# Gate projections with tokens on partitions, turned through DRAM; small transfers on GpSimd's queue; one square per tile

## The chip, the core and the metric

The kernel runs on one core of a Trainium2 chip, as one launch. The metric is device time in microseconds; the median of three runs before the change is 1785.23 us (1784.16 to 1788.43). The core has a matrix engine (PE, whose weight loads the profile lists as PEld), VectorE (DVE), ScalarE (ACT), GpSimd (POOL) and a sync engine (SP). DMAs are issued from the queues of SP, ACT and POOL. All engines run their own instruction streams in order and wait for each other through semaphores.

## The reference

Two layers over 256 latent tokens and 256 context tokens, all in float32 with 2048 channels. The first layer is the one that the change touches:

```
p  = h @ w_in                      # 256 x 14400: q, gate_a, z, k, v, x/B/C of the scan, dt
pc = hc @ w_in[:, COL_K:]
q, k = rms_norm over each head's 128 channels of p's q and k columns
ya = neighbourhood_attention(q, k, v, kc, vc, rpb) * silu(gate_a)      # 16 heads of 128
y_ssd = bidirectional_ssd(...)                                         # 8 groups of 4 heads of 64
yb = gated_group_rmsnorm(y_ssd + d * xs, z, g)      # y * silu(z), then a norm over each group's 256
x  = x + gate * (concat(ya, yb) @ w_out)
```

The second layer is a gated short convolution: `(silu(g) * bg * conv(cg * hv)) @ w_out`. The modulation rows (shift, scale, gate) of both layers come from a matrix-vector product with `ada_w`.

## The kernel before

**Precision.** Every large product is made from float32r halves: each operand is split into a high part (a cast) and a low part (what the cast lost), and three matmuls are summed, high by high, high by low and low by high. For a weight chunk of 128 x 1024 the cast `wH` is ACT's (line 427) and the subtraction `wL` is DVE's (line 434). Three chunks may be split ahead of use (`NW = 3`). `hH`, `hL` are the halves of the modulated input, `mix` those of the mixed heads before the output projection, `h` and `y` those of the second layer.

**Two layouts.** A projection is called with a kind. With `"act"`, `mm_act` puts tokens on partitions: an activation block of 128 x 128 is stationary, 512 weight columns move, and the result is a bank of 128 tokens x 512 channels for each 128 tokens. With a number, `mm_ws` puts channels on partitions: the weight block is stationary, and 256 or 512 tokens move. Q, K and V are projected with `"act"`; the scan's X and B with 512 moving tokens; C, the attention gate G and the scan's gate Z with 256 (only latent tokens have gates). The attention and the scan want gates with channels on partitions, in the tiles `gt` and `sz`, four blocks of 128 channels by 256 tokens. So Q and K have to be turned and G and Z need not.

**The turn through DRAM.** `kq_gen` squares Q or K on ACT head by head (four activations with an accumulated sum per tile), takes the power -1/2 on POOL, scales on DVE into `tmp` tiles with the 32-channel pieces shuffled (`mixed`, `plain`), and writes each tile to a DRAM scratch (`kqd`) by a DMA from POOL. `fetch` reads it back by four DMAs from POOL (line 214), each for 32 partitions, into the tile of tag `PT0`; `blocks` (line 219) finishes the turn with 32 x 32 block transposes on DVE. The same path turns the softmax's result (`ptd`, tile `D`) and, in the second layer, `trd` (tiles `Du`, `Dg`). All first-layer fetches share the one `PT0` buffer: `dfree` is true when it may be taken.

**Stages.** For a = 0 to 3 (four heads each) and s = 0 to 3 (two scan groups each), the first layer projects Q and K, then G and V, then C, X, Z of the scan; for a = 3 the scan comes between. Each projection's tail is a generator: `kq_gen`, `silu2_gen` (for G and Z: tanh on ACT, product on DVE, straight into `gt` or `sz`), `v_gen`, `head_gen` for one head, `make_x` and `group_gen` for the scan. A finished row block of `mix` whose place is still held by `hH` or `hL` is parked in DRAM (`put_mix`, `mixd`) and fetched later (`mix_gen`). `gemv_gen` makes the modulation rows on DVE (`acc`, line 826) in between and writes them to `mrow`. The parking, the modulation rows and the scan's decay rows (`csr`, `exr`) go by ACT's DMA queue (`DMA2`).

**What sets the order.** The program is written out while a planner (`Plan`) keeps a modelled clock for every engine. A generator yields what it needs next, `W_(engine, tiles)`, and `pump` emits the next step of the first generator in the queues `urgent`, `side`, `back` whose operands the model thinks ready in time. `cap` and `grow` change how many `tmp` and `half` tiles a generator may hold. The model decides only where an instruction stands in its engine's stream; on the chip semaphores decide when it runs.

Of the kernel before, what the change touches and what calls it, by code (L numbers as in the profile page):

```python
# [14 lines left out]
D = 2048  # L15
# [128 lines left out]
def kernel(ctx: ExitStack, tc, x, cx, ada_w, ada_b, w_in, w_out, sc_in, sc_out, rpb, small, const,  # L144
# [211 lines left out]
    def give(pool, *bs):  # L356
        pool.extend(bs)
# [451 lines left out]
    def gemv_gen():  # L809
        for n in range(16):  # L810
            lay = 0 if n < 4 else 1
            c0 = 4096 + n * 512 if n < 4 else (n - 4) * 512
            yield W_("SP")
            E(DMA.dma_start(adab[0:128:32, :], ada_b[lay, c0:c0 + 512].rearrange("(g c) -> g c", g=4)))
            for k in range(8):
                yield when(lambda: not (("gem", n, k) not in RAW))
                yield W_("DVE+", RAW["gem", n, k][1])
                raw, v = RAW.pop(("gem", n, k))
                ngem[0] -= 1
                for j in range(2):  # L820
                    if j:
                        yield W_("DVE", acc)
                    if not k + j:
                        E(V.tensor_scalar(out=acc, in0=v[:, j], scalar1=csil[:, 0:1], scalar2=None, op0=ALU.mult))
                        continue
                    E(V.scalar_tensor_tensor(out=acc, in0=v[:, j], scalar=csil[:, 2 * k + j:2 * k + j + 1], in1=acc,  # L826
                                             op0=ALU.mult, op1=ALU.add))
# [9 lines left out]
            yield W_("AQ", rowb)  # L837
            E(DMA2.dma_start(mrow[n // 4, (n % 4) * 512:(n % 4) * 512 + 512].rearrange("(g c) -> g c", g=4), rowb[0:128:32, :]))
            n_back[0] = n
            if n == 11:  # L840
                yield W_("AQ", mrow[2:3, 1024:])
                E(DMA2.dma_start(mrb[:32, :], mrow[1:3, :].rearrange("r (b c) -> (r b) c", c=128)))
# [132 lines left out]
    def kq_gen(key, a, ps, nt, stat, dst, banked):  # L975

        for t in range(nt):
            yield W_("ACT", ps[t])
            jk = tmp()
            for h in range(4):  # L980
                E(S.activation(jk[:, h * 128:h * 128 + 128], ps[t][:, h * 128:h * 128 + 128], AF.Square,
                               accum_out=stat[:, 4 * t + h:4 * t + h + 1]))
            give(free_t, jk)
        yield W_("DVE", stat)
        rstd(stat[:, :4 * nt], stat[:, :4 * nt], 128, EPS, 4 * nt)
        src = kqd[a, 512 * (key == "Q"):512 * (key == "Q") + 128 * nt]

        for t in range(nt):
            yield W_("DVE", stat)
            kn = tmp()  # L990
            E(V.tensor_tensor(out=mixed(kn), in0=plain(ps[t]),
                              in1=stat[:, 4 * t:4 * t + 4].unsqueeze(2).unsqueeze(3).to_broadcast([128, 4, 4, 32]), op=ALU.mult))
            if banked:
                give(free_b, ps[t])
            yield W_("POOL", kn)
            E(G.dma_start(src[t * 128:(t + 1) * 128], kn))
            give(free_t, kn)
# [12 lines left out]

    def v_gen(a, ps):
# [4 lines left out]
            give(free_b, ps[t])  # L1016
        got.add(("V", a))

    def silu2_gen(key, a, ps, dst, ok):
# [12 lines left out]
    b0 = rpbs[0, :, :]  # L1032
# [6 lines left out]
    def head_gen(a, h):  # L1039
# [32 lines left out]
        def scale_(qt):  # L1072
            yield W_("DVE", s4[:, 4 + qt:5 + qt])
            E(V.reciprocal(s4[:, 6 + qt:7 + qt], s4[:, 4 + qt:5 + qt]))
            yield W_("ACT", s4[:, 6 + qt:7 + qt])
            E(S.mul(sps[qt], sps[qt], s4[:, 6 + qt:7 + qt]))
            yield W_("POOL", sps[qt])
            E(G.dma_start(ptd[hd, qt * 128:(qt + 1) * 128], sps[qt]))
            give(free_t, sps[qt])
# [17 lines left out]
        yield from top(1, p1)  # L1097
        for qt in range(2):
            yield from scale_(qt)
        yield ("cap", 0, 0)  # L1100
# [43 lines left out]
    def dt_gen(ps):  # L1144
# [86 lines left out]
        yield W_("AQ", rw)  # L1231
        E(DMA2.dma_start(csr, rw[:64, 0:256]))
        E(DMA2.dma_start(exr, rw[:64, 256:512]))
        give(free_t, rw)
        got.add("dt")

# [251 lines left out]

    def do_g(a, nxt):
        psG = banks(2)  # L1490
        proj(512, 256, psG, nxt)
        spawn(urgent, silu2_gen("G", a, psG, gt, lambda: attn[0] >= 8 * a and (a or ("K", 0) in got)), 1)

    def do_ssd(s, nxt):
        if s:
            psB = banks(2)
            proj(256, 512, psB, 1)
            spawn(urgent, make_b(s, psB), 3)
        psC, = banks(1)
        proj(256, 256, [psC], 4)  # L1500
        spawn(urgent, make_c(s, psC), 0, 2)
        psX = banks(4)
        proj(512, 512, psX, 2)
        for gi in range(2):
# [3 lines left out]
        spawn(urgent, silu2_gen("Z", s, psZ, sz, lambda: ssd_done[0] >= 2 * s and ("K", 0) in got), 1)  # L1508
        for gi in range(2):
            spawn(side, group_gen(s, gi), 3, 4)  # L1510

# [39 lines left out]
    def mix_gen(ip):  # L1551
        two_ = (2 * ip, 2 * ip + 1)
        yield when(lambda: all(i in written or mH[i] is not None for i in two_) and free_rows[0] > (2 * ip + 1) % 16)
        mine = [i for i in two_ if mH[i] is None]
        if not mine:
            return
        yield ("grow", 1, 0)
        yield W_("AQ", *[mixd[i] for i in mine])
        mx = tmp()
        m3 = two(mx)  # L1560
        if len(mine) == 2:
            E(DMA2.dma_start(m3, mixd[2 * ip:2 * ip + 2].rearrange("b p c -> p b c")))
        else:
            E(DMA2.dma_start(m3[:, mine[0] % 2], mixd[mine[0]]))
# [221 lines left out]
    def row_gen(i, pC, pH):  # L1786
# [7 lines left out]
        for t in range(2):  # L1794
# [7 lines left out]
            give(free_t, ut)  # L1802
# [21 lines left out]
    def gate_gen(i, pB, pG):  # L1824
# [7 lines left out]
        for t in range(2):  # L1832
# [12 lines left out]
            give(free_t, o)  # L1845
# [114 lines left out]
```

## Time and profile before

| | |
|---|---|
| median of the runs | 1785.23 us |
| the profiled execution | 1781.03 us, span 1779.2 us |
| PE busy | 1736.7 us, 98% of the span |
| DVE, ACT, POOL busy | 1278.5, 799.0, 160.3 us (72%, 45%, 9%) |
| DMA | 412.51 MB, 232 GB/s over the span |
| chain that ended last | PE 71%, issue 10%, DMA 8%, DVE 7% |

"Busy" is the time in which at least one instruction of an engine ran. Consecutive matmuls overlap in the records, so the cost of a matmul in a stream is the distance between two starts, and not its own duration. The groups of instructions count by source line, operation and tile; most matmuls have line 200, since one helper records them all.

### The profile page before, as it was taken

How to read it: one execution, taken by the hardware profiler on the slowest of the kernel's cores; microseconds unless marked ns; L12 is line 12 of the kernel's file. 1: busy time of each engine (PE TensorE's matmuls, PEld its weight loads, DVE VectorE, ACT ScalarE, POOL GpSimd, SP SyncE). 2: the span in 40 equal slices, each digit the busy share in tenths (PEclk: the TensorE clock that was granted, in tenths of full speed). 3: DMA queues.
4: the chain of work that ended last, by engine and by line, in shares of the span. 5: the costliest groups of instructions: out<-in, count | busy, mean ns of one | idle time of the engine just before them, and what ended most of it. 6: DMA issues, size and time to landing. Idle time of an engine off the chain costs nothing.

```text
span 1779.2 us, 25400 instructions
## 1 busy us (share of the span) xinstructions
PE 1736.7 (98%) x9305; PEld 1445.1 (81%) x9305; DVE 1278.5 (72%) x2017; ACT 799.0 (45%) x1354; POOL 160.3 (9%) x245
## 2 busy tenths in 40 slices
PE   6999999999999999999999999999999999999998
PEld 4677988888788879788878898787878887878887
DVE  5566777878786876686887688776667776766555
ACT  5422444464344454343454445654435444444442
POOL 0000211012101012101012100010000000000000
PEclk9999999999999999999999999999999999999999
DMA  9987776677776678766578658777766887877775
GB/s 340 341 293 253 215 210 190 188 225 238 231 226 202 178 235 251 235 191 214 173 243 237 202 162 235 228 239 263 256 220 223 273 280 247 261 252 217 218 223 167
DMA packets 259742, 412.51 MB, mean 232 GB/s; under 512 B 35968, under 2 KB 105376, under 8 KB 259616
## 3 DMA queue, kind: packets, MB, share of 16 engines
q1 hardware_dynamic: 239888, 366.64, 66.5%
q0 software_dynamic: 12672, 37.76, 6.6%
q10 hardware_dynamic: 7056, 6.47, 1.1%
q8 instruction: 73, 1.20, 0.3%
q14 instruction: 53, 0.43, 0.1%
HBM read 386.53 MB, written 25.59 MB: 232 GB/s over the span
## 4 chain that ended last, share of the span: by engine, by line
PE 71%; issue 10%; DMA 8%; DVE 7%; POOL 2%; ACT 1%; SPq 1%; DVEq 0%; ACTq 0%; POOLq 0%
PE bank L200 70%; DMA raw<-in_ada_w 3%; DVE wL L434 2%; PE bank L204 1%; DMA raw<-in_w_in 1%; DMA dram_trd<-tmp 1%; DVE acc L826 1%; DMA bias<-dram_rpbs 1%; DMA kqD_K<-dram_kqd 1%; DMA D<-dram_ptd 1%; ACT wH L427 1%; DMA Du<-dram_trd 1%; POOL statk L576 0%; POOL kqD_K L214 0%; POOL Dg L214 0%
## 5 line engine op out<-in xcount | busy, mean ns | idle before, releaser
L427 ACT CAST wH<-raw 128x1024 fp32r<-128x1024 f32 (+1 forms) x440 | 459.4, 1045 | 650.9 <-PE bank L200 553.2
L434 DVE TENSOR_TENSOR wL<-raw,wH 128x1024 fp32r<-128x1024 f32 (+1 forms) x440 | 532.0, 1213 | 240.4 <-ACT wH L427 235.9
L200 PE MATMUL bank<-hH,wH 128*128 128x256 f32 (+1 forms) x1040 | 341.4, 328 | 0.9 <-ACT wH L427 0.9
L200 PE MATMUL bank<-hL,wH 128*128 128x256 f32 (+1 forms) x1040 | 337.2, 324 | 0.0
L200 PE MATMUL bank<-hH,wL 128*128 128x256 f32 (+1 forms) x1024 | 331.6, 324 | 0.6 <-DVE wL L434 0.6
L200 PE MATMUL bank<-wH,h 128*128 128x512 f32 x1024 | 318.4, 391 | 2.1 <-DVE h L1693 1.7
L200 PE MATMUL bank<-wH,hH 128*128 128x512 f32 x640 | 256.7, 402 | 4.8 <-ACT hH L767 2.6
L200 PE MATMUL bank<-wL,hH 128*128 128x512 f32 x640 | 250.5, 392 | 0.3 <-DVE wL L434 0.3
L200 PE MATMUL bank<-wH,hL 128*128 128x512 f32 x640 | 249.8, 391 | 0.1
L200 PEld LDWEIGHTS bank<-wH,h 128*128 128x128 f32 x1024 | 192.7, 188 | 44.3 <-DVE h L1693 3.0
L200 PEld LDWEIGHTS bank<-hH,wH 128*128 128x128 f32 x1040 | 198.1, 190 | 18.4 <-issue 2.0
L200 PEld LDWEIGHTS bank<-hL,wH 128*128 128x128 f32 x1040 | 198.2, 191 | 15.2
L826 DVE SCALAR_TENSOR_TENSOR acc<-raw,csil,acc 128x512 f32<-128x512 f32 x240 | 179.3, 747 | 41.1 <-DMA raw<-in_ada_w 37.3
L200 PEld LDWEIGHTS bank<-hH,wL 128*128 128x128 f32 x1024 | 194.9, 190 | 17.2 <-DVE wL L434 1.5
L200 PE MATMUL bank<-wL,h 128*128 128x512 f32 x512 | 200.4, 391 | 3.7 <-DVE wL L434 3.7
L200 PE MATMUL bank<-wH,mix 128*128 128x512 f32 x512 | 160.1, 390 | 0.0
L200 PEld LDWEIGHTS bank<-wH,hH 128*128 128x128 f32 x640 | 120.6, 188 | 36.5 <-issue 7.4
L200 PEld LDWEIGHTS bank<-wH,hL 128*128 128x128 f32 x640 | 120.5, 188 | 25.7 <-DVE hL L773 0.6
L200 PEld LDWEIGHTS bank<-wL,hH 128*128 128x128 f32 x640 | 120.6, 188 | 24.4 <-DVE wL L434 0.7
L200 PEld LDWEIGHTS bank<-wL,h 128*128 128x128 f32 x512 | 96.5, 188 | 25.3 <-DVE wL L434 5.3
L200 PEld LDWEIGHTS bank<-wH,mix 128*128 128x128 f32 x512 | 96.1, 188 | 20.2 <-issue 0.4
L200 PE MATMUL bank<-wL,mix 128*128 128x512 f32 x256 | 99.8, 390 | 0.0
(271 smaller groups left out, 1849.1 us busy)
## 6 DMA issues: line engine op xcount, KB each, us to landing
raw<-in_w_in SPq DMA_DIRECT2D x209, 512.0 KB
raw<-in_ada_w SPq DMA_DIRECT2D x163, 512.0 KB
raw<-in_sc_in SPq DMA_DIRECT2D x128, 512.0 KB
raw<-in_w_out SPq DMA_DIRECT2D x64, 512.0 KB
raw<-in_sc_out SPq DMA_DIRECT2D x32, 512.0 KB
dram_ptd<-tmp POOLq DMA_DIRECT2D x32, 256.0 KB, 4.1
D<-dram_ptd POOLq DMA_DIRECT2D x64, 128.0 KB, 4.9
tmp<-dram_csr SPq DMA_DIRECT2D x32, 256.0 KB
```

Of the source, the lines that this page charges most:

```text
L200: E(T.matmul(o, l, r, start=start, stop=stop, skip_group_check=True))
L204: E(T.transpose(o, i, ident if k == 128 else ident[:k, :k]))
L427: E(S.copy(H, v))
L434: E(V.tensor_tensor(out=Lo, in0=v, in1=H.bitcast(F32), op=ALU.subtract))
L826: E(V.scalar_tensor_tensor(out=acc, in0=v[:, j], scalar=csil[:, 2 * k + j:2 * k + j + 1], in1=acc, op0=ALU.mult, op1=ALU.add))
```

## The change

1. **G and Z are projected with `"act"`**, as Q and K are. `silu2_gen` makes the gate with tokens on partitions in `tmp` tiles, writes two tiles to a new DRAM scratch `gzd` from POOL, fetches them back into the `PT0` buffer by the four DMAs of `fetch`, and turns them by `blocks` on DVE into `gt` or `sz`. The columns of G and Z in `w_in` are permuted on the host so that the shuffle of 32-channel pieces is already made. `head_gen` takes `PT0` for its softmax only once its gate is there.
2. **ACT's DMA queue is no longer used**: the writes of `mrow`, its one read, the parked `mix` blocks and their reads, `csr` and `exr` are issued by POOL.
3. **One square per tile**: ACT squares a tile of 128 x 512 at once, DVE sums it per head.
4. **Tiles of a DMA are given back later**: a `tmp` or `half` tile that a POOL DMA reads counts as free only when the model has the DRAM tile written.

```
     def put_mix(i, o):
...
-        yield W_("AQ", o)
-        E(DMA2.dma_start(mixd[i], o))
+        yield W_("POOL", o)
+        E(G.dma_start(mixd[i], o))
+        yield W_("POOL", mixd[i])
         give(free_h, o)
...
     def kq_gen(key, a, ps, nt, stat, dst, banked):
...
-            for h in range(4):
-                E(S.activation(jk[:, h * 128:h * 128 + 128], ps[t][:, h * 128:h * 128 + 128], AF.Square,
-                               accum_out=stat[:, 4 * t + h:4 * t + h + 1]))
+            E(S.activation(jk, ps[t], AF.Square))
+            yield W_("DVE", jk)
+            E(V.tensor_reduce(out=stat[:, 4 * t:4 * t + 4], in_=four(jk), axis=AX.X, op=ALU.add))
...
     def silu2_gen(key, a, ps, dst, ok):
-        yield when(lambda: ok())
-        for b in range(2):
-            yield W_("ACT", ps[b])
+        ths = []
+        src = gzd[4 * (key == "Z") + a]
+        for t in range(2):
+            yield W_("ACT", ps[t])
             th = tmp()
-            E(S.activation(th, ps[b], AF.Tanh, scale=0.5))
+            E(S.activation(th, ps[t], AF.Tanh, scale=0.5))
             yield W_("DVE", th)
-            E(V.scalar_tensor_tensor(out=dst[:, 2 * b:2 * b + 2, :].rearrange("p b c -> p (b c)"), in0=th, scalar=1.0,
-                                     in1=ps[b], op0=ALU.add, op1=ALU.mult))
-            give(free_t, th)
-            give(free_b, ps[b])
+            E(V.scalar_tensor_tensor(out=th, in0=th, scalar=1.0, in1=ps[t], op0=ALU.add, op1=ALU.mult))
+            give(free_b, ps[t])
+            yield W_("POOL", th)
+            E(G.dma_start(src[t * 128:(t + 1) * 128], th))
+            ths.append(th)
+        yield W_("POOL", src)
+        give(free_t, *ths)
+        yield ("cap", 0, 0)
+        yield when(ok)
+        yield when(lambda: dfree[0])
+        Dt = d_take(f"D{key}{a}")
+        yield W_("POOL", src)
+        fetch(Dt, src)
+        for t in range(2):
+            yield W_("DVE+", Dt)
+            blocks(dst[:, :, t * 128:(t + 1) * 128], Dt[:, t])
+        dfree[0] = True
         got.add((key, a))
...
-        yield when(lambda: dfree[0] and (hd == 0 or ("d", hd - 1) in got))
+        yield when(lambda: dfree[0] and ("G", a) in got and (hd == 0 or ("d", hd - 1) in got))
...
-        proj(512, 256, psG, nxt)
+        proj(512, "act", psG, nxt)
...
-        proj(512, 256, psZ, nxt)
+        proj(512, "act", psZ, nxt)
...
     def mix_gen(ip):
...
-            E(DMA2.dma_start(m3, mixd[2 * ip:2 * ip + 2].rearrange("b p c -> p b c")))
+            E(G.dma_start(m3, mixd[2 * ip:2 * ip + 2].rearrange("b p c -> p b c")))
```

Three places show how the streams change. The first is PE at the border from the projection of K to that of G for a = 1. In the names `bank` is a PSUM bank, the operand after the arrow that comes first is the moving one, and the numbers are the tile's instance. Before:

```order
L200 MATMUL bank_123<-wH_138,hH_1437 128x512
L200 MATMUL bank_123<-wL_141,hH_1437 128x512
L200 MATMUL bank_123<-wH_138,hL_1442 128x512
L200 MATMUL bank_128<-hH_362,wH_136 128x256
L200 MATMUL bank_128<-hL_366,wH_136 128x256
L200 MATMUL bank_128<-hH_362,wL_139 128x256
```

After:

```order
L200 MATMUL bank_126<-wL_141,hH_1437 128x512
L200 MATMUL bank_126<-wH_138,hL_1442 128x512
L200 MATMUL bank_123<-wH_136,hH_362 128x512
L200 MATMUL bank_123<-wL_139,hH_362 128x512
L200 MATMUL bank_123<-wH_136,hL_366 128x512
```

For one block of 128 input channels, four times three matmuls of 256 columns became two times three of 512, with the operands' roles exchanged.

The second place is POOL's queue at the turn of Q and K for a = 1 (`kqD` are the fetches of Q and K, `D` those of a head, `DG` that of the gate, `ptd` and `gzd` writes of softmax tiles and gates, `r` and `statk` the powers -1/2). Before:

```order
L1467 TENSOR_TENSOR r_1_1706<-r_1_1706,const 128x2
L214 DMA kqD_Q_3809<-dram_kqd 32x8x128 x4
L214 DMA kqD_K_3867<-dram_kqd 32x8x128 x4
L214 DMA kqD_K_3922<-dram_kqd 32x8x128 x4
L1078 DMA dram_ptd<-tmp_113 128x512
L1078 DMA dram_ptd<-tmp_105 128x512
L214 DMA D_4055<-dram_ptd 32x8x128 x4
```

After:

```order
L1488 TENSOR_TENSOR r_0_1706<-r_0_1706,const 128x2
L959 DMA dram_mixd<-half_115 128x256
L214 DMA kqD_K_3497<-dram_kqd 32x8x128 x4
L959 DMA dram_mixd<-half_118 128x256
L214 DMA kqD_K_3587<-dram_kqd 32x8x128 x4
L1488 TENSOR_TENSOR r_1_1707<-r_1_1707,const 128x2
L838 DMA dram_mrow<-rowb 4x128
L959 DMA dram_mixd<-half_114 128x256
L214 DMA DG_3635<-dram_gzd 32x8x128 x4
```

A third fetch joins the two of K, parked blocks stand between them, and the power of a scan group now stands behind a fetch.

The third place is DVE at the same turn, where `KT` and `gt` are what the transposes fill, `acc` the modulation rows and `kL`, `qL` the first head's low parts. Before:

```order
L434 TENSOR_TENSOR wL_141<-raw_131,wH_138 128x1024
L219 STREAM_TRANSPOSE KT<-kqD_K_3867 128x4x4x32 x2
L826 SCALAR_TENSOR_TENSOR acc<-raw_132,csil,acc 128x512 x2
L826 SCALAR_TENSOR_TENSOR acc<-raw_134,csil,acc 128x512 x2
L434 TENSOR_TENSOR wL_139<-raw_133,wH_136 128x1024
L826 SCALAR_TENSOR_TENSOR acc<-raw_132,csil,acc 128x512 x2
L219 STREAM_TRANSPOSE KT<-kqD_K_3922 128x4x4x32 x2
```

After:

```order
L219 STREAM_TRANSPOSE KT<-kqD_K_3587 128x4x4x32 x2
L826 SCALAR_TENSOR_TENSOR acc<-raw_132,csil,acc 128x512
L434 TENSOR_TENSOR wL_139<-raw_131,wH_136 128x1024
L1106 TENSOR_TENSOR kL<-KT,kH 128x512
L1107 SCALAR_TENSOR_TENSOR qL<-QT,gqk,qH 128x256
L826 SCALAR_TENSOR_TENSOR acc<-raw_134,csil,acc 128x512 x2
L1083 ISA tmp_111,s_0_1694<-bank_123,bias_213 128x512
L1083 ISA s_0_1694 128x1
L1086 TENSOR_SCALAR s_0_1694<-s_0_1694 128x1
L826 SCALAR_TENSOR_TENSOR acc<-raw_132,csil,acc 128x512 x2
L219 STREAM_TRANSPOSE gt<-DG_3635 128x4x4x32 x2
L434 TENSOR_TENSOR wL_140<-raw_135,wH_137 128x1024
```

The gate's two transposes join the row of turns, directly ahead of a weight chunk's `wL`; between them and K's last pair stands one `wL` and the first head's work.

More of the change, by code (lines that the diff above doesn't have):

```diff
@@ L836, in gemv_gen @@
             give(free_b, ps)
-            yield W_("AQ", rowb)
-            E(DMA2.dma_start(mrow[n // 4, (n % 4) * 512:(n % 4) * 512 + 512].rearrange("(g c) -> g c", g=4), rowb[0:128:32, :]))
+            yield W_("POOL", rowb)
+            E(G.dma_start(mrow[n // 4, (n % 4) * 512:(n % 4) * 512 + 512].rearrange("(g c) -> g c", g=4), rowb[0:128:32, :]))
             n_back[0] = n
             if n == 11:
-                yield W_("AQ", mrow[2:3, 1024:])
-                E(DMA2.dma_start(mrb[:32, :], mrow[1:3, :].rearrange("r (b c) -> (r b) c", c=128)))
+                yield W_("POOL", mrow[2:3, 1024:])
+                E(G.dma_start(mrb[:32, :], mrow[1:3, :].rearrange("r (b c) -> (r b) c", c=128)))
                 yield W_("PE", mrb, nb=1)
@@ L996, in kq_gen @@
             E(G.dma_start(src[t * 128:(t + 1) * 128], kn))
-            give(free_t, kn)
+            kns.append(kn)
+        yield W_("POOL", src)
+        give(free_t, *kns)
         yield ("cap", 0, 0)
@@ L1099, in head_gen @@
             yield from scale_(qt)
+        yield W_("POOL", ptd[hd])
+        give(free_t, sps[0], sps[1])
         yield ("cap", 0, 0)
-        yield when(lambda: dfree[0] and (hd == 0 or ("d", hd - 1) in got))
+        yield when(lambda: dfree[0] and ("G", a) in got and (hd == 0 or ("d", hd - 1) in got))
         Dt = d_take(f"D{hd}")
@@ L1230, in dt_gen @@
         give(free_b, pr)
-        yield W_("AQ", rw)
-        E(DMA2.dma_start(csr, rw[:64, 0:256]))
-        E(DMA2.dma_start(exr, rw[:64, 256:512]))
+        yield W_("POOL", rw)
+        E(G.dma_start(csr, rw[:64, 0:256]))
+        E(G.dma_start(exr, rw[:64, 256:512]))
         give(free_t, rw)
@@ L1490, in do_g @@
         psG = banks(2)
-        proj(512, 256, psG, nxt)
-        spawn(urgent, silu2_gen("G", a, psG, gt, lambda: attn[0] >= 8 * a and (a or ("K", 0) in got)), 1)
+        proj(512, "act", psG, nxt)
+        spawn(urgent, silu2_gen("G", a, psG, gt, lambda: attn[0] >= 8 * a and (a or ("K", 0) in got)), 2)
     def do_ssd(s, nxt):
@@ L1506, in do_ssd @@
         psZ = banks(2)
-        proj(512, 256, psZ, nxt)
-        spawn(urgent, silu2_gen("Z", s, psZ, sz, lambda: ssd_done[0] >= 2 * s and ("K", 0) in got), 1)
+        proj(512, "act", psZ, nxt)
+        spawn(urgent, silu2_gen("Z", s, psZ, sz, lambda: ssd_done[0] >= 2 * s and ("K", 0) in got), 2)
         for gi in range(2):
@@ L1557, in mix_gen @@
         yield ("grow", 1, 0)
-        yield W_("AQ", *[mixd[i] for i in mine])
+        yield W_("POOL", *[mixd[i] for i in mine])
         mx = tmp()
@@ L1801, in row_gen @@
             E(G.dma_start(trd[2 * i, t * 128:(t + 1) * 128], ut))
-            give(free_t, ut)
+            cs[t] = ut
+        yield W_("POOL", trd[2 * i])
+        give(free_t, *cs)
         yield ("cap", 0, 0)
@@ L1844, in gate_gen @@
             E(G.dma_start(trd[2 * i + 1, t * 128:(t + 1) * 128], o))
-            give(free_t, o)
+            gs[t] = o
+        yield W_("POOL", trd[2 * i + 1])
+        give(free_t, *gs)
         yield ("cap", 0, 0)
@@ L1942 @@
     strict = np.stack([lt.T, lt], axis=1)
+    w_in = np.array(f('na_ssd_w_in')[0])
+    w_in[:, COL_G:COL_K] = w_in[:, COL_G:COL_K].reshape(D, 8, 4, 4, 32).transpose(0, 1, 3, 2, 4).reshape(D, 4096)
     arr = {
-        'x': f('x')[0], 'cx': f('ctx')[0], 'ada_w': f('ada_w'), 'ada_b': f('ada_b'), 'w_in': f('na_ssd_w_in')[0],
+        'x': f('x')[0], 'cx': f('ctx')[0], 'ada_w': f('ada_w'), 'ada_b': f('ada_b'), 'w_in': w_in,
         'w_out': f('na_ssd_w_out')[0], 'sc_in': f('sc_w_in')[0], 'sc_out': f('sc_w_out')[0], 'rpb': f('na_rpb')[0],
```

6 lines of the change are left out of this document (4 added, 2 removed).

## The prediction

> **What bounds the kernel now.** I read the page first, then PE's waits, then the distances of matmul starts in the timeline, then the queue that the change loads most, POOL.
>
> ```profile
> span 1779.2 us, 25400 instructions
> PE 1736.7 (98%) x9305; PEld 1445.1 (81%) x9305; DVE 1278.5 (72%) x2017; ACT 799.0 (45%) x1354; POOL 160.3 (9%) x245
> PEclk9999999999999999999999999999999999999999
> ...
> 175.00:1480.00 1305.00, 1292.41 (x6962) 1096.04 (x6961) 988.47 (x1580) 604.30 (x1081) 139.12 (x203) 1.00 0.73 223
> ```
>
> The last row is from the busy time by stretches: from 175 us, where the start-up ends, to 1480 us PE is busy for 1292.41 of 1305.00 us at the full granted clock (1.00). So PE bounds the kernel, only 12.6 us of that stretch are gaps, and time can be won in two ways: fewer or shorter matmuls, or those gaps. The waits of PE say what the gaps are:
>
> ```profile
> PE bank L200 <- DVE wL L434: 4.6, 7, 1.8
> PE bank L200 <- ACT qH L1085: 2.7, 2, 1.6
> PE bank L200 <- DVE tmp L1431: 2.3, 1, 2.3
> PE bank L200 <- DVE half L1454: 1.1, 1, 1.1
> PE bank L200 <- DVE PL L1115: 0.7, 2, 0.4
> ```
>
> They are few and short (total, times, longest): a late weight chunk here, a late first head there. DVE at 72% and ACT at 45% are not bounds, but PE depends on both in order.
>
> **The matmuls (the one term on the path).** How many there are of G's and Z's kind is in the groups by shape, and what one costs is the distance of starts:
>
> ```profile
> L200 PE MATMUL bank<-hH,wH 128*128 128x256 f32 x640 | 182.7, 286 | 0.0
> ...
> 299.83 0.28 PE L200 MATMUL bank<-hL,wH 128*128 128x256 f32 x1
> 302.95 0.28 PE L200 MATMUL bank<-hH,wH 128*128 128x256 f32 x1
> ...
> 389.65 0.39 PE L200 MATMUL bank<-wL,hH 128*128 128x512 f32 x1
> 398.72 0.39 PE L200 MATMUL bank<-wH,hL 128*128 128x512 f32 x1
> ```
>
> Between 299.83 and 302.95 us lie 26 distances in one unbroken stream of 256-column matmuls: 3.12/26 = 0.1200 us each. Between 389.65 and 398.72 us lie 40 distances of the "act" form with 512 columns: 9.07/40 = 0.2268 us each. Two of the short ones cost 0.2400, one long one 0.2268: 13.2 ns are saved per pair. The 640 matmuls of the row, times three halves, are 1920; C keeps 4 x 16 x 2 x 3 = 384 of them, so G and Z have 1536, which become 768 of 512 columns. 768 x 0.0132 = 10.2 us. Since PE is dense at both places, I count all of it as on the path.
>
> A rule of the Trainium skill speaks for less. Its page "TensorE: Matmul & The Clock Gate", section "Back-to-back issue gap", gives a warm matmul N/2.4 + 2.5 ns; by it 768 matmuls fewer would save only 768 x 2.5 ns = 1.9 us. The two rows differ by 106.8 ns for 256 columns, which agrees with the page's slope, but leave 13 ns, not 2.5, as the fixed part, so the measurement decides.
>
> **ACT.** The squares and the queue:
>
> ```profile
> L981 ACT ACTIVATE tmp<-bank 128x128 f32<-128x128 f32 x80 | 20.9, 308 | 0.0
> L981 ACT ACTIVATION_READ_ACCUMULATOR tmp<-bank 128x1 f32 x80 | 18.5, 240 | 0.0
> L605 ACT ACTIVATE tmp<-xs 128x512 f32<-128x512 f32 x8 | 5.0, 624 | 2.9 <-DMA xs<-in_x 2.7 <-DMA xs<-in_cx 0.2
> ACT wH L427 <- issue: 56.2, 25, 5.4
> ```
>
> The 80 squares and 80 reads of 20 tiles take 39.4 us, with the four tiles in `sz` and `gt` 47 us at the same price; 24 squares of 512 at 0.624 us take 15.0. ACT loses 32 us of work and 55 DMA issues. I cost it at nothing: ACT is idle over half of the time, and the cover stays. Whether the waits of the fourth row ("issue": ended by nothing that the profile shows, 25 times) were the queue's DMAs, and whether PE felt them, is open; PE's waits on ACT after the start-up are 2.7 (row of qH) and some below 1 us. Bounds 0 to -3 us; I take 0.
>
> **DVE.** It gets 16 block transposes and 24 sums of 128 x 512:
>
> ```profile
> L219 DVE STREAM_TRANSPOSE KT<-kqD_K 128x512 f32<-128x512 f32 x16 | 10.4, 689 | 10.5 <-DMA kqD_K<-dram_kqd 10.5
> L219 DVE STREAM_TRANSPOSE QT<-kqD_Q 128x512 f32<-128x512 f32 x8 | 5.2, 688 | 0.0
> L824 DVE TENSOR_SCALAR acc<-raw,csil 128x512 f32<-128x512 f32 x16 | 7.6, 475 | 3.8 <-DMA raw<-in_ada_w 3.8
> L826 DVE SCALAR_TENSOR_TENSOR acc<-raw,csil,acc 128x512 f32<-128x512 f32 x240 | 179.3, 747 | 41.1 <-DMA raw<-in_ada_w 37.3
> ```
>
> The transposes cost 16 x 0.689 = 11.0 us. No row shows a sum of 512; rows of that size lie between 475 and 747 ns, and I take the transpose's 0.689: 24 x 0.689 = 16.5 us. DVE comes to 1278.5 + 27.5 = 1306 us, 73%. The gate's own two operations stay as long as they were (the same 128 x 512). Cover: PE's work; if DVE were the bound of a stage, this would be the price, which is why the bounds are 0 and 27.5 us. Since PE's waits on `wL` add up to 4.6 us in seven times at 72% load, I take 0 for the work itself and put the waits into the next term.
>
> **POOL and the new turns.** POOL gets 16 writes and 32 fetch DMAs of gates, 24 parked blocks and 12 reads of them, 17 of the modulation rows and 2 of the decay rows: 103 DMAs.
>
> ```profile
> L214 POOL DMA_DIRECT2D D<-dram_ptd x64 | 37.7, 592 | 212.7 <-DVE PL L1115 102.5 <-DVE tmp L1372 58.5 <-issue 41.5
> L1078 POOL DMA_DIRECT2D dram_ptd<-tmp x32 | 17.9, 559 | 198.1 <-ACT tmp L1076 170.3 <-ACT tmp L1413 21.5 <-DMA raw<-in_w_in 4.0
> ```
>
> At 0.56 to 0.59 us each that is 60 us; POOL comes to 220 us, 12%. What counts is waiting in order, and the second layer shows it in one piece. POOL's rows, then DVE's, then PE's:
>
> ```profile
> 1473.03 1.77 POOL L214 DMA_DIRECT2D Du<-dram_trd  x3 [6.26 <-DMA dram_trd<-tmp]
> 1480.52 0.58 POOL L214 DMA_DIRECT2D Du<-dram_trd  x1 [5.72 <-issue]
> 1486.52 1.30 DVE L219 STREAM_TRANSPOSE u<-Du 128x512 f32<-128x512 f32 x2 [2.67 <-DMA Du<-dram_trd]
> 1493.17 2.35 DVE L434 TENSOR_TENSOR wL<-raw,wH 128x1024 fp32r<-128x1024 f32 x2
> 1494.45 0.50 PE L200 MATMUL bank<-wL,h 128*128 128x512 f32 x1 [1.79 <-DVE wL L434]
> ```
>
> Three DMAs of a fetch are issued at once, the fourth only 5.72 us later; the data land at 1486.4; DVE has stood for 2.67 us; the `wL` queued behind comes late, and PE stands for 1.79 us. Every new fetch can do this: behind the gate's transposes stand `wL` (the order's third place), on POOL the next head's fetch and a scan group's power. It need not:
>
> ```profile
> DVE KT L219 <- DMA kqD_K<-dram_kqd: 10.5, 4, 6.5
> DVE D L1109 <- DMA D<-dram_ptd: 7.4, 5, 2.7
> DVE u L219 <- DMA Du<-dram_trd: 5.2, 2, 2.7
> ```
>
> DVE waited at 4 of 8 fetches of K, 5 of 16 of a head, 2 of 4 of `u`, and at none of Q (0.0 in its row above). PE's waits that can come from a turn are `wL` 4.6, `qH` 2.7, `PL` 0.7, together 8.0 us, and there are 36 fetches: 0.22 us each. Bounds for one new fetch: 0 (as for Q) to 1.79 us (as above); for eight 0 to 14.3. I take 0.3 us each, a little over the mean, since G's and Z's fetches share one buffer and one queue with more DMAs than before: 2.4 us.
>
> The traffic, 8 x 1.05 MB written and read back in 412.5 MB, is 2% more at a DMA share of 0.73; SP's loads keep their order but for single places. I cost it at nothing: PE waited for a weight load from DRAM only in the start-up, which the change leaves as it was. Tiles held longer cost nothing by themselves either: they move where an instruction stands, and where one lacks, a side generator starts later behind PE's projections; without that cover it would show as a gap of the size of a landing, and such gaps are in the bounds above. The second layer's matmuls are untouched.
>
> **The sum.** 1781.0 (profiled execution) - 10.2 + 2.4 = 1773.2 us. The median of the runs is 4.2 us above the profiled execution, so in the runs 1785.2 - 7.8 = 1777.4, say 1777 us.
>
> **Rivals.**
>
> *More is won.* ACT's waits were the queue's and PE's small gaps go with them: besides the 10.2, `qH` 2.7 and `half`, `tmp` (1.1 and 2.3), none of it lost to new turns: 1785.2 - 10.2 - 6.1 = 1769 us. For it: 25 unexplained waits, on the engine that makes `wH`. Against: the gaps at these places name three engines.
>
> *The gain is eaten.* The new turns cost about 1 us each: 1785.2 - 10.2 + 8 = 1783 us, no change by the bound of 0.3% (5.4 us) that a measurement of this kernel can tell. For it: K, the fetch most like the new one (a buffer that is waited for, its transposes ahead of `wL`), had waits at half of its fetches.
>
> *Slower.* One mechanism: POOL's queue. The fourth DMA of a fetch waits until earlier ones are through, the writes now put ahead lengthen this, and everything on POOL behind it (a head's fetch, a group's power) comes late too. It decides if twelve fetches, the eight new ones and four old ones that now have a write directly ahead, cost the 1.79 us of the row: 21.5 us, so 1785.2 - 10.2 + 21.5 = 1796 us; slower by 0.3% from 15.6 us on. Against: POOL is at 12%, and a single write costs it 0.56 us. The Trainium skill speaks for it: "SBUF — State Buffer", section "SBUF: two separate sides", says that DMAs issued by GpSimd can starve for descriptors while DVE runs certain operations, and advises ACT's or SP's queue. The trace shows no slow issue, 592 ns on average beside a DVE at 72%; only the fourth waits.
>
> *The shapes cost alike.* If the 13 ns were not per matmul but of something that stays with G and Z (other operands, other neighbours), only the new turns would be left: 1785.2 + 2.4 = 1788 us. Against it stand 40 distances of the very form that is put in. The Trainium skill's formula above comes out near this case, with 1.9 us saved: 1786 us.
>
> **Chances and range.** My forecast, 1772 to 1780 us, 0.50; more is won 0.17; eaten 0.18; slower 0.11; the shapes cost alike 0.04. Faster by over 0.3% means below 1779.9: 0.48 of the first and all of the second, 0.65. Slower means above 1790.6: 0.11 and a hundredth of the others, 0.12. The rest, 0.23, is no change. The range leaves about 0.1 on each side: 1767, below the second case, to 1789, above "eaten" and "cost alike" and short of the slow one.
>
> **What would show it.** Right: 768 matmuls fewer, 512 columns at 0.227 us where 256 stood; PE's busy time from 175 to 1480 us down by some 10 us; POOL near 220 us; DVE near 1306, ACT near 767 us; waits of DVE on `DG` or `DZ` of a few us in all. Wrong: PE waits on `wL` or `qH` well over the 8 us above (the turns cost more), DVE's sums far over 0.75 us, gaps of PE behind POOL's powers, or a `kH,qH` product that stands earlier in PE's stream than its K can be there.

## The result and the profile after

The changed kernel takes 1797.27 us (median, 1790.3 to 1800.98) against 1784.7 us before: a ratio of 1.0068, 95% interval [1.0049, 1.0087]. It is slower by 12 us; forecast was 1777 us. The profiled execution took 1798.02 us, 17.0 us more than the one of before. From the page and from the busy time by stretches of after (columns: window, length, busy time of PE, PEld, DVE, ACT, POOL, granted clock, DMA share, GB/s):

```profile
span 1796.2 us, 23892 instructions
PE 1736.8 (97%) x8537; PEld 1411.1 (79%) x8537; DVE 1304.2 (73%) x2057; ACT 785.6 (44%) x1186; POOL 219.8 (12%) x348
...
175.00:1480.00 1305.00, 1273.74 (x6095) 1046.14 (x6094) 995.74 (x1597) 581.45 (x904) 193.88 (x298) 0.99 0.74 224
```

768 matmuls have gone, yet PE is busy as long as before, and the gaps from 175 to 1480 us have grown from 12.6 to 31.3 us. I split the distances of all matmul starts: if each is set to the median of its kind (tile names and shape), the sum falls from 1680 to 1670 us, by 10 us; what is over that by more than 0.25 us at a time, stalls, rises from 36.5 to 55.6; excesses of 0.03 to 0.25 us rise from 52.7 to 59.7. So the matmuls' gain is there, and 26 us were lost beside it. PE's waits of after (total, times, longest):

```profile
PE bank L200 <- DVE wL L434: 10.5, 14, 2.5
PE bank L200 <- ACT Vt L1019: 7.1, 1, 7.1
PE bank L200 <- DVE tmp L1452: 3.6, 5, 1.3
PE bank L200 <- ACT qH L1104: 3.5, 1, 3.5
PE bank L204 <- POOL r L1488: 3.1, 1, 3.1
```

`wL` has gone from 4.6 to 10.5, and three single stalls of 3 to 7 us are new. The longest shows how a stall comes about. POOL, then DVE, ACT and PE, in the timeline of after (start, duration, and in brackets the idle time before):

```profile
1128.25 0.76 POOL L1583 DMA_DIRECT2D tmp<-dram_mixd  x1
1135.87 0.72 POOL L1583 DMA_DIRECT2D tmp<-dram_mixd  x1 [6.87 <-issue]
1135.68 0.71 DVE L1130 STREAM_TRANSPOSE D<-D 128x512 f32<-128x512 f32 x1 [7.40 <-DMA D<-dram_ptd]
1137.69 1.06 ACT L1134 CAST PH<-D 128x1024 fp32r<-128x1024 f32 x1 [10.26 <-DVE D L1130]
1148.93 2.02 ACT L1019 COPY Vt<-bank 128x512 f32<-128x512 f32 x4
1149.56 1.19 PE L200 MATMUL bank<-tmp,xtm 128*64 128x128 f32 x8 [7.11 <-ACT Vt L1019]
```

DVE stood 7.4 us for a head's `D`, ACT stood 10.3 us for DVE, and the copies of `Vt` that free V's banks stood behind that in ACT's order; PE waited 7.1 us for them. POOL's wait of 6.87 us stands behind that `D` and not ahead of it: the fetch's fourth DMA was issued at 1126.25 us and landed 9.3 us later, while its other three had landed after 2.6 to 3.4 us. PE then ran at half clock:

```profile
1149.00:1150.00 1.00, 0.44 (x4) 0.44 (x6) 0.00 (x0) 1.00 (x4) 0.02 (x1) 0.50 0.89 211
1150.00:1152.00 2.00, 2.00 (x11) 1.48 (x8) 0.00 (x0) 1.58 (x3) 1.99 (x3) 0.50 0.72 231
```

The records of the granted clock show 0.5 for 3.4 or 6.8 us at a time, mostly at stalls of 1.8 us or more. Between 175 and 1700 us that is 7 us in all before and 27 us after. Half of the difference, 10 us, is the most that it can have cost by this estimate; of the small excesses, 2.9 us lie in such stretches before and 9.4 us after, which is most of the 7 us by which they rose. The Trainium skill, "TensorE: Matmul & The Clock Gate", section "What's actually happening", describes such a gate, with an activity window of about 3.4 us; the lengths of the stretches agree. It lets the clock fall after an idle window of that length, and here stalls of 1.8 us (before, at 1494 us) and 2.5 us (after, at 245 us) were enough.

### The profile page after: what moved, and what is told of

It reads as the page before. It is cut to its first block, busy times and chain, and to the rows that moved or that the text cites. A ratio compares the mean times of both kernels' runs of the same rounds, so it can differ in the third digit from the quotient of the medians.

```text
span 1796.2 us, 23892 instructions
## 1 busy us (share of the span) xinstructions
PE 1736.8 (97%) x8537; PEld 1411.1 (79%) x8537; DVE 1304.2 (73%) x2057; ACT 785.6 (44%) x1186; POOL 219.8 (12%) x348
## 5 line engine op out<-in xcount | busy, mean ns | idle before, releaser
L200 PE MATMUL bank<-wH,hH 128*128 128x512 f32 x896 | 360.3, 403 | 4.8 <-ACT hH L767 2.6
L200 PE MATMUL bank<-wL,hH 128*128 128x512 f32 x896 | 351.9, 393 | 0.8 <-DVE wL L434 0.8
L200 PE MATMUL bank<-wH,hL 128*128 128x512 f32 x896 | 351.3, 393 | 0.1
L200 PEld LDWEIGHTS bank<-wH,hH 128*128 128x128 f32 x896 | 169.8, 190 | 45.7 <-issue 6.6
L200 PE MATMUL bank<-hH,wH 128*128 128x512 f32 (+1 forms) x528 | 195.6, 370 | 0.9 <-ACT wH L427 0.9
L200 PE MATMUL bank<-hH,wL 128*128 128x512 f32 (+1 forms) x512 | 187.4, 366 | 5.9 <-DVE wL L434 5.9
L200 PE MATMUL bank<-hL,wH 128*128 128x512 f32 (+1 forms) x528 | 192.7, 365 | 0.0
L200 PEld LDWEIGHTS bank<-hH,wL 128*128 128x128 f32 x512 | 97.2, 190 | 23.3 <-DVE wL L434 7.8
L200 PEld LDWEIGHTS bank<-hH,wH 128*128 128x128 f32 x528 | 100.3, 190 | 18.0 <-issue 2.0
L200 PEld LDWEIGHTS bank<-hL,wH 128*128 128x128 f32 x528 | 100.4, 190 | 14.9
```

The costliest lines, as they stand in the source:

```text
L200: E(T.matmul(o, l, r, start=start, stop=stop, skip_group_check=True))
```

## Experiments

Ratios are to the kernel before, run beside each, so rows are compared by their ratios; the medians come from several chips. 0.1% is 1.8 us. All rows marked "2k" have the doubled DMA scratch of the first experiment. Seven kernels leave out the gates' turn or its DMAs, so that `gt` and `sz` hold no turned gate: `ring2k_noturn`, `noturn_traffic`, `order_alone` and the four whose names begin with `act_`.

| kernel | median us | ratio, 95% interval |
|---|---|---|
| after_ring2k (2k) | 1786.72 | 1.0018 [1.0006, 1.0030] |
| before_ring2k (2k) | 1785.16 | 1.0007 [0.9993, 1.0021] |
| no_queue | 1806.71 | 1.0128 [1.0110, 1.0147] |
| no_gates | 1780.97 | 0.9982 [0.9967, 0.9998] |
| gates_only | 1802.93 | 1.0127 [1.0098, 1.0155] |
| ring2k_traffic (2k) | 1802.74 | 1.0138 [1.0106, 1.0171] |
| ring2k_knows (2k) | 1784.56 | 1.0018 [1.0003, 1.0033] |
| ring2k_r260 (2k) | 1786.47 | 1.0033 [1.0013, 1.0053] |
| ring2k_noturn (2k) | 1789.07 | 1.0024 [1.0003, 1.0044] |
| noturn_traffic (2k) | 1789.06 | 1.0027 [1.0017, 1.0037] |
| no_gates_ring2k (2k) | 1777.47 | 0.9960 [0.9946, 0.9974] |
| no_gates_traffic (2k) | 1779.82 | 0.9985 [0.9970, 1.0000] |
| act_direct (2k) | 1769.95 | 0.9938 [0.9915, 0.9960] |
| act_transposes (2k) | 1788.09 | 1.0031 [1.0014, 1.0047] |
| order_alone (2k) | 1788.59 | 1.0040 [1.0020, 1.0061] |
| act_direct_unplanned (2k) | 1771.60 | 0.9941 [0.9924, 0.9959] |
| act_direct_r260 (2k) | 1775.73 | 0.9969 [0.9952, 0.9986] |
| ring2k_blind (2k) | 1792.65 | 1.0055 [1.0033, 1.0078] |

**1. The room for POOL's DMAs.** The order of every engine stays as it was.

```
-    sb.tile([128, 224], F32, tag="pad", name="pad", bufs=1)
+    sb.tile([128, 4], F32, tag="pad", name="pad", bufs=1)
-    nc = bacc.Bacc("TRN2", ..., dynamic_dma_scratch_size=1024)
+    nc = bacc.Bacc("TRN2", ..., dynamic_dma_scratch_size=2048)
```

> The changed kernel with POOL's DMA scratch doubled from 1024 to 2048 (an unused filler tile gives the room); every engine's instructions stay in the same order. Theory A, the loss is POOL waiting for room in that scratch: POOL's waits ended by 'issue' ahead of fetches and of the read of parked blocks (158.6 us in sum after, 102.4 before) fall below 60 us, PE's stalls over 0.25 us (55.6 us in sum after, 36.5 before) fall to about 35, half-clock time in the middle goes from 27 us back to 7, and the time falls from 1797 to 1775 to 1783 us. Rival B, the loss is the gates' turn itself (its transposes ahead of wL, the extra sums, the traffic): the time stays 1793 to 1800 us whatever POOL's waits do.

> The kernel before with the same doubled scratch, instruction order unchanged. Theory A: the wait of each fetch's fourth DMA is a wait for room, so the 5.72 us ahead of Du's fourth DMA and most of the 102 us go, PE's gaps behind Du (1.8 us twice) with them; 1779 to 1783 us against 1785. Rival B, the fourth DMA waits for something else (for the landing of the first, or a fixed pace of POOL): POOL's waits stay at about 100 us and the time at 1785 within 2 us.

POOL's waits ended by nothing that the profile shows, of after, then of after with the doubled scratch; with each, VectorE's waits for the heads' `D`:

```profile
POOL D L214 <- issue: 49.2, 22, 7.1
POOL dram_gzd L1036 <- issue: 29.3, 1, 29.3
POOL kqD_K L214 <- issue: 27.4, 10, 5.7
POOL DZ L214 <- issue: 16.2, 5, 4.0
POOL tmp L1583 <- issue: 10.0, 3, 6.9
DVE D L1130 <- DMA D<-dram_ptd: 22.0, 6, 7.4
```

```profile
POOL dram_gzd L1036 <- issue: 29.8, 2, 29.6
POOL DZ L214 <- issue: 4.1, 1, 4.1
POOL Du L214 <- issue: 3.8, 1, 3.8
POOL D L214 <- issue: 1.0, 4, 0.3
DVE D L1130 <- DMA D<-dram_ptd: 4.5, 3, 2.5
```

The wait of a fetch's fourth DMA is a wait for room in that scratch: it goes when the scratch is doubled, while POOL's issues and DVE's load (73%) stay. The one long wait at a gate's write (`dram_gzd`) stays too, so it is something else; the page does not tell what. With the room, VectorE's waits for `D` fall from 22.0 to 4.5 us (7.4 in the kernel before). In after the lack of room costs 0.50%, 9 us (10.6 by the medians); in the kernel before the same waits (102 us of POOL) go as well, as this row of it with the doubled scratch shows (41.5 us before), and nothing is won:

```profile
POOL D L214 <- issue: 1.6, 4, 0.6
```

My expectation of 1775 to 1783 us was too low: something else costs more. The Trainium skill's "SBUF — State Buffer", section "SBUF: two separate sides", says that DMAs of GpSimd can starve while DVE runs certain operations. No run here shows that: the waits went with DVE as busy as ever.

**2. Which part loses.** Part 2 undone (all of its DMAs back on `DMA2`, waits on `"AQ"`); part 1 undone (`silu2_gen` and both `proj` calls as before); and part 1 alone.

> The changed kernel with part 2 undone: parked blocks, their reads, modulation rows and decay rows go by ACT's queue again; gates, squares and the later give-back stay. Theory A, POOL's queue is full because of part 2 and part 1 together and the stop at 1127 to 1160 us comes from the reads of parked blocks there: 1776 to 1786 us. Rival B, the gates' turns lose it: 1792 to 1800 us. Rival C, the queue on ACT costs what was moved away: 1797 or more.

> The changed kernel with part 1 undone: G and Z projected with 256 moving columns straight into gt and sz, no new turn; small transfers on POOL, one square per tile and later give-back stay. PE has the 10 us of matmuls more again. Theory A (part 2 on POOL loses most, with or without gates): 1795 to 1805 us. Rival B (the gates' turns lose it): 1783 to 1788 us. If both are needed to fill POOL's scratch: 1785 to 1792 us.

> The kernel before with part 1 alone: G and Z projected with tokens on partitions and turned through DRAM; ACT's queue, the four squares a tile and the early give-back as before, scratch 1024. Theory A, part 1 is what loses and parts 2 to 4 only soften it: 1795 to 1808 us, POOL's waits by 'issue' near 180 us as with part 2 undone, PE busy in matmuls 10 us less. Rival B, part 1 needs the other parts to lose (their sums, the later give-back): 1775 to 1788 us.

Theory A on part 2 falls: without it the changed kernel is slower, by 0.6%, 9 us by the medians, and POOL's waits stay (the `D` row reads 47.9 us there). So part 2 does not lose it; whether it helps by the queue itself or by the order that is planned with it is not shown. Without the gates, parts 2 to 4 win 0.2%, 3 us. Part 1 alone loses 1.27%. So the gates lose it, by 0.86% or 15 us against the kernel without them, although they save PE 10 us.

**3. Bytes, or the planner's view of them.**

```
+            G.dma_start(dump[8 * (key == "Z") + 2 * a + t], w_out[0:256, 0:512])   # ring2k_traffic
...
+                if e == "POOL":                                                    # ring2k_knows
+                    self.dma = max(self.dma, s + 1000) + n / self.RATE
...
-    RATE = 270.0                                                                   # ring2k_r260
+    RATE = 260.0
```

> The changed kernel with the doubled scratch and, unknown to the planner, one DRAM-to-DRAM copy of 512 KB from POOL behind each of the 16 writes of a gate, 8.4 MB in all: the gates' traffic once more with no new dependence; the engines' order stays otherwise (16 POOL issues more). Theory T, what is left of the loss with the doubled scratch (1786.7, 16 us over the kernel without the gates less its 10 us of matmuls) is traffic, which makes ada_w's loads late where the DMA engines are 0.9 busy: VectorE's waits on them rise from 58 to over 75 us and the time by 8 to 16 us, to 1795 to 1803. Rival U, traffic is hidden and the order loses it: at most 3 us more, 1785 to 1790.

> The changed kernel with the doubled scratch, and a planner that counts the bytes of POOL's DMAs against the weight loads that follow (before, it takes them as free). Theory T, loads are later than planned and VectorE stands in order on ada_w: the waits on ada_w fall below 40 us and the time to 1772 to 1781 us. Rival U: another order like any other, 1784 to 1792 us.

> The changed kernel with the doubled scratch, the planner's rate of weight loads set from 270 to 260 bytes per ns: a slightly other order everywhere. It measures how much a mere reordering moves: if orders are worth 2 or 3 us, 1784 to 1790; if theory T holds and planned loads were too early, it goes part of the way, 1778 to 1784.

The copies cost 16 us by the medians, 1.2% by the ratios, as theory T wanted, which made me believe it. But VectorE's waits on `ada_w` between 175 and 1340 us rose only from 57.9 to 67.8 us, and the planner that counts bytes brought them down to 34.1 us, as wanted, and won nothing. The next four runs took the theory apart.

**4. The turn's DMAs left out.** In the first kernel the gates' writes and fetches are only planned, and the transposes read `KT`; the second adds the copies.

```
-            E(G.dma_start(src[t * 128:(t + 1) * 128], th))
+            plan.add(None, fake=("POOL", "DMACopy", [th], [src[t * 128:(t + 1) * 128]]))
...
-        fetch(Dt, src)
+        for b in range(4):
+            plan.add(None, fake=("POOL", "DMACopy", [src], [Dt[32 * b:32 * b + 32]]))
...
-            blocks(dst[:, :, t * 128:(t + 1) * 128], Dt[:, t])
+            # the same transpose from KT[:, 2 * t], planned as if from Dt
```

> The changed kernel with the doubled scratch, where the gates' 16 writes and 32 fetch DMAs are left out and their 16 transposes read KT instead (so gt and sz hold no gate); PE, ACT and SP keep their order, VectorE does the same work. Theory T, the 16 us left with the doubled scratch are the 8.4 MB: 1768 to 1775 us, half-clock time in the middle 7 to 11 us. Rival U, VectorE's extra work and the planner's order lose them: 1782 to 1787 us. In between: they share it.

> The same kernel without the turn's DMAs, with 16 DRAM-to-DRAM copies of 512 KB from POOL where the writes stood: the 8.4 MB are back, with nothing that waits for them. Theory T: 1783 to 1790 us again. Rival V, what costs is the waiting for the turn (landing, PT0, POOL's order), not the bytes: it stays within 4 us of the kernel without the turn.

> Parts 2 to 4 of the change without the gates, scratch doubled. If the scratch costs only where gates are turned: within 2 us of 1781. If its waits still cost there (POOL's issue waits 144 us): 1776 to 1779, the fastest so far.

> The last kernel with 16 DRAM-to-DRAM copies of 512 KB (8.4 MB) from POOL behind the products of the gates, of which nothing depends. Theory T: the bytes alone cost 10 to 18 us, 1791 to 1799. Rival V: up to 4 us, 1780 to 1785.

Theory T falls. Without the turn's DMAs nothing is won (1.0024 against 1.0018), and 8.4 MB put back cost nothing there (1.0027) and 0.25%, or 2 us by the medians, in the kernel without gates. Why the same copies cost 16 us beside the real turn stays open; there the traffic is twice the change's, and between 175 and 1340 us ACT waited for the weights of `w_in` 30.9 us instead of 18.2. The fastest kernel so far came out of this: parts 2 to 4 with the doubled scratch.

**5. From that kernel to the changed one in single steps.** `act_direct` projects G and Z with `"act"` in the fastest kernel and writes the product straight into `gt` and `sz`; `act_transposes` adds 16 planned transposes; `order_alone` is `ring2k_noturn` with the transposes only planned, too.

```
-        proj(512, 256, psG, nxt)                 # act_direct, and for psZ
+        proj(512, "act", psG, nxt)
...
+        for t in range(2):                       # act_transposes, behind the products
+            yield W_("DVE+", dst)
+            blocks(dst[:, :, t * 128:(t + 1) * 128], KT[:, 2 * t])
...
+            plan.add(None, fake=("DVE", "StreamTranspose", [i], [o]))   # order_alone, in place of each transpose
```

> Parts 2 to 4 with the doubled scratch (1777.5 us), and G and Z projected with tokens on partitions but the product written straight into gt and sz as before, without a turn (so gt and sz hold the gate unturned): the term of the matmuls by itself. Theory M, the 10.2 us of matmuls are on the path: 1765 to 1769 us. Rival N, PE's gain is given back because something else sets the pace at those places (weights, VectorE's queue): 1774 to 1779 us. Rival O, a mere change of matmul shape makes the planner's order worse: 1780 or more.

> The same with 16 transposes of KT into gt and sz behind the products (VectorE's part of the turn, without its DMAs and without planned waits for them). Theory W, VectorE's 11 us of transposes ahead of wL cost PE: 8 to 12 us more than the kernel without them. Rival: hidden, within 3 us of it, and then the planned wait for the turn, which shifts heads and scan groups, is what costs.

> The changed kernel with the doubled scratch and the planner's order of the turn, but neither its 48 DMAs nor its 16 transposes are issued (gt and sz hold a constant): PE, ACT and SP in the same order as with the turn (1786.7 us; 1789.1 without the DMAs). Theory P, the order that comes from planning the turn is what costs: 1783 to 1790 us, with the stalls at the same places (729 to 734, 1118, 1147 us). Theory W, VectorE's transposes cost: 1775 to 1780 us.

The step is in the order. `order_alone` issues none of the turn's DMAs or transposes, runs as many instructions as `act_direct` on every engine but for two more on VectorE that set the constant, and is 1.0% slower, 18 us. From 175 to 1470 us, of `act_direct` and of `order_alone`:

```profile
175.00:1470.00 1295.00, 1281.48 (x6177) 1054.73 (x6176) 1003.03 (x1604) 589.62 (x912) 169.59 (x257) 1.00 0.74 225
```

```profile
175.00:1470.00 1295.00, 1269.48 (x6090) 1043.08 (x6089) 987.26 (x1583) 581.97 (x904) 165.06 (x250) 0.99 0.73 219
```

12 us more gaps in the same stretch, with VectorE less busy. Over the whole span PE is also busy 6.5 us longer (1734.1 for 1727.6 us) with the same matmuls, and the half clock covers 20 for 10 us from 175 to 1700 us. In this order PE's longer stalls are the same ones with and without the turn. PE in the timeline of the changed kernel with the doubled scratch, then of `order_alone` (its lines are shifted: L1461 is the same as L1452, L1113 as L1104, L1024 as L1019):

```profile
734.28 0.50 PE L200 MATMUL bank<-kH,qH 128*128 128x512 f32 x1 [2.98 <-ACT qH L1104]
1119.19 0.65 PE L200 MATMUL bank<-tmp,xtm 128*64 128x128 f32 x6 [3.11 <-DVE tmp L1452]
1147.09 0.73 PE L200 MATMUL bank<-tmp,xtm 128*64 128x128 f32 x8 [2.92 <-ACT Vt L1019]
```

```profile
734.26 0.80 PE L205 MATMUL bank<-kH,qH 128*128 128x512 f32 x1 [2.98 <-ACT qH L1113]
1119.66 1.11 PE L205 MATMUL bank<-tmp,xtm 128*64 128x128 f32 x6 [4.12 <-DVE tmp L1461]
1146.62 1.19 PE L205 MATMUL bank<-tmp,xtm 128*64 128x128 f32 x8 [2.16 <-ACT Vt L1024]
```

These three are 9.3 us together in `order_alone`; in `act_direct` PE waits 0.9 us for `qH` from 175 to 1700 us, and not for `Vt` or that `tmp`. So the stall of 7.1 us that I first read as POOL's has two parts: its place comes from the order (2 to 3 us there with no turn at all), and the scratch's wait made it longer. What the order did there, the tile's rows show: the last scan groups' products with `xtm` (first and last start), of `act_direct`, `order_alone` and after:

```profile
L200 PE MATMUL bank<-tmp,xtm x32: 272/273/323, 1096.3 to 1130.1; 128*64 128x128 f32 x32
```

```profile
L205 PE MATMUL bank<-tmp,xtm x32: 272/323/474, 1115.1 to 1185.2; 128*64 128x128 f32 x32
```

```profile
L200 PE MATMUL bank<-tmp,xtm x32: 272/298/476, 1116.7 to 1194.1; 128*64 128x128 f32 x32
```

They end 55 and 64 us later, among the matmuls of the output projection. That the late tails, with less beside them to cover, are why PE waits there is my reading. It cannot be the whole cause: in `act_transposes`, which is about as slow as `order_alone`, these products run from 1108.9 to 1140.3 us, and in `act_direct_r260` (experiment 6), which is fast, from 1107.6 to 1163.2 us. Other orders with a planned turn also stall at other places (`ring2k_blind` longest, 4.5 us, at 934 us), which were not followed.

**6. Is it VectorE's work, or luck?** 16 transposes of `KT` in the unchanged order of `act_direct`, unknown to the planner; `act_direct` with a rate of 260; and the real turn with the gates' transposes unplanned (`V.transpose` in place of `blocks`).

> The kernel that writes the unturned gate directly (1770.0 us), in exactly its order on PE, ACT, POOL and SP, with 16 transposes of KT into gt and sz put on VectorE behind the products without the planner's knowledge. Theory P, the order costs and not VectorE's 11 us: 1769 to 1774 us. Theory W, the 11 us are paid wherever they run: 1780 to 1788 us, as with the planned transposes (1788.1).

> The kernel that writes the unturned gate directly, planned with a rate of 260 instead of 270: another order of the same work. If the fast time was one lucky order, 1776 to 1787 us; if the work without a turn allows it in general, 1767 to 1774 us.

> The changed kernel with the doubled scratch and its real turn, but a planner that does not count the gates' 16 transposes on VectorE (their place in the program is the same step, the DMAs are planned as before). Theory P: the order becomes like that without the turn, 1771 to 1779 us, faster than both kernels. Rival: the other waits of the turn (scratch, PT0, heads after their gate) make the order what it is: 1783 to 1789 us.

VectorE's 11 us of transposes cost 0.03% in the good order, 2 us by the medians: they are hidden. Two orders without a turn are 0.9938 and 0.9969; four with the planned or half-planned turn are 1.0018, 1.0018, 1.0033 and 1.0055, and `act_transposes` and `order_alone` lie among them. The groups do not touch, nor do their intervals, but each spreads over 0.3 to 0.4%, 6 us. So the order costs between 0.5% and 1.2%, depending on which two are compared. My repair failed: leaving the transposes out of the plan did not bring the good order back, and `act_transposes`, which plans the transposes and nothing else of the turn, was as slow as the rest. Which of the turn's planned pieces (VectorE's time, the `tmp` tiles held, the shared `PT0`, heads after their gate) makes the order bad is not settled; either of two seems enough.

## Why the prediction was wrong, point by point

- **The matmuls, -10.2 us: right in size.** In the trace they are -10 us, so the rival of equal cost falls. That all of it is on the path is not shown: from `no_gates_ring2k` to `act_direct` the runs give 0.22%, 4 us, with intervals that overlap, and an order moves 6 us. The formula that I took from the Trainium skill, "TensorE: Matmul & The Clock Gate", section "Back-to-back issue gap", is called there the gap of an isolated matmul, so it was no price for a stream of weight loads and matmuls such as this one.
- **ACT at nothing: right, with a wrong size.** ACT fell by 13.4 us, not 32: a square and the read of its accumulator overlap, and I had added their rows (47 us for the 24 tiles), where the line is busy for 26.6 us. The 25 unexplained waits of `wH` were not the queue's DMAs: ACT issues none now, and there are more of them:

```profile
ACT wH L427 <- issue: 71.7, 31, 5.4
```

- **DVE's work at nothing: right.** 1304.2 us were forecast as 1306; a sum takes 0.677 us for the 0.689 taken; the transposes are hidden (experiment 6). So is the traffic at the change's own size.

```profile
L983 DVE TENSOR_REDUCE statk<-tmp 128x4 f32<-128x512 f32 x16 | 9.9, 677 | 0.0
L219 DVE STREAM_TRANSPOSE gt<-DG 128x512 f32<-128x512 f32 x8 | 5.2, 689 | 1.4 <-DMA DG<-dram_gzd 1.4
```

- **POOL and the new turns, +2.4 us: this step failed.** I priced a turn by what VectorE and PE had waited for landings, 0.3 us each. The gates' own landings are indeed cheap (VectorE waited 1.4 us for `DG`, 2.8 for `DZ`). But the lack of room in POOL's scratch cost 9 us, and I had priced it at the new fetches alone. POOL's waits at fetches and reads of parked blocks rose from 102 to 159 us, 40 of the 56 at the gates' fetches and those reads; what VectorE paid stands at an old fetch: its waits for `D` are 22.0 us, 7.4 before (those for K fell from 10.5 to 2.6). Two of the signs named for being wrong came: PE waited 14.0 us for `wL` and `qH`, and 3.1 us behind a scan group's power. The slower rival named this queue, at 21.5 us for twelve fetches; the mechanism was right, the size more than double. That its 1796 us lies beside the measured 1797 is luck: it counted this queue at more than double, and the order, which it did not count, made up for that and for more.
- **"They move where an instruction stands": the larger failure.** Held tiles and moved steps were costed at nothing, with the bounds of one fetch as their cover. The new order alone costs 18 us (1.02%, and 0.5 to 1.2% among the orders run), nearly twice the matmuls' 10 us and more than the bounds of all eight fetches, 14.3 us. PE's stalls for `qH`, `tmp` and `Vt` are 9.3 us of it; which of the turn's planned pieces moves them stays open.
- **A stall was counted once.** Half clock behind it costs up to 1.7 us more per stretch of 3.4 us, by estimate; that such stretches would grow from 7 to 27 us was not in the sum.

In ratios, one step after another, the 0.68%: parts 2 to 4 -0.18, more scratch -0.22, the matmuls -0.22, the order +1.02, the transposes run -0.16 and the turn's DMAs -0.06 (both no difference by their intervals), the scratch taken back +0.50. The order's step and the last one are clear of noise; at the -0.22 of the scratch and of the matmuls the intervals overlap.

The best version with all of the computation is `no_gates_ring2k`: parts 2 to 4 without the gates, with the doubled scratch, 1777.47 us, 0.4% faster than before and 1.1% faster than the change.

## What to carry to other kernels

Where a planner writes the order, price a new step in two parts: what it runs, and what the order does to everything else. The second can be measured alone, by planning the step without issuing it, and two or three runs with a slightly changed planner's constant tell how much any order is worth (here up to 6 us), below which a single part's gain should not be believed; the matmuls' 4 us in the runs is such a gain. When a queue waits for nothing that the profile shows, change the room that it has before blaming what was put into it.

## What was not expected of the hardware

- With POOL's scratch of 1024 two or three of a fetch's four DMAs are issued at once; the next, or a DMA of another kind, waits (49.2 us in 22 waits at `D`, 7.1 us at most). With 2048 the waits at `D` fall to 1.0 us, which is worth 0.50% in the changed kernel and nothing in the kernel before (1.0007).
- A stall of PE of 1.8 us or more mostly comes with half clock for 3.4 or 6.8 us. It is no sharp rule: a stall of 2.3 us in the kernel before has none (1117 us), and there is one behind stalls of 0.2 to 0.4 us (761 us).
- 8.4 MB copied from DRAM to DRAM by POOL cost 0 to 4 us in two kernels with a DMA share of 0.74, and 16 us by the medians beside the turn, at a share of 0.76; why is open.
